# Giving product M5 of a GELU MLP its second Strassen level, with chained PSUM sums and claimed result tiles, on one Trainium2 core

## The chip, the cores and the metric

The kernel runs on one core of one Trainium2 chip. The metric is the device time of one execution in microseconds (us); a quoted time is the median of several executions. Every run quoted here is fast: the mean granted TensorE clock of a run was 0.996 or higher. Ratios are the mean time of one kernel's fast runs over that of the other's fast runs of the same rounds, so they are not quite the ratio of the medians beside them.

The engines are named as the profile names them: PE is TensorE (PEld its weight loads), DVE is VectorE, ACT is ScalarE, POOL is GpSimd, and SP is the engine whose queue issues the loads.

## The reference

```python
x: (8, 1024, 1024)   w1: (1024, 4096)   w2: (4096, 1024)   # float32
h = x @ w1
h = 0.5 * h * (1 + np.tanh(np.sqrt(2 / np.pi) * (h + 0.044715 * h ** 3)))
return (h @ w2).astype(np.float32)
```

## The kernel before

The 8192 rows are worked on in eight superblocks (SB 0 to 7) of 1024 rows. Each has a first matmul (`x @ w1`, then GELU, result `g` in fp16) and a second (`g @ w2`). Each of these is one level of Strassen's method: seven products M1 to M7 of half-size blocks in place of eight.

In the second matmul of SB 2 to 7 five of the seven products (M1, M2, M3, M6, M7) are split once more: an inner Strassen product makes seven quarter-size multiplications of 16 matmuls with 256 columns, so 112 x 256 columns instead of 64 x 512. M4 and M5 are still plain. A split product needs four more operand sums (made by VectorE during the product before it) and four more weight sums (made once, early, and kept in HBM as `in_d[m]`).

The inner product before, which the change rewrites; `ab`, `bb`, `cb` are PSUM banks, `tt` is a VectorE add or subtract, `act_copy` a ScalarE copy:

```python
def steps(self, into):
    ...
    ab, bb, cb = psum(), psum(), psum()
    self.multiply(1, ab, True);  v = temp(); act_copy(v, ab)              # step 1
    self.multiply(6, bb, True);  tt(c12, pair(v), pair(bb), ADD, True)    # 2
    self.multiply(2, ab, False); act_copy(c11, pair(ab))                  # 3
    self.multiply(7, bb, False); tt(c21, pair(v), pair(bb), ADD, True)    # 4
    self.multiply(5, cb, True);  tt(c22, c21, pair(cb), ADD, True)        # 5
    self.multiply(4, ab, True);  tt(c21, c21, pair(ab), SUB, True)        # 6
    self.multiply(3, cb, False); tt(c12, c12, pair(cb), ADD, True)        # 7
    # (cut: the storing of finished parts, the hand-over after each step, and, in the last
    # superblock, M7's base tile, with three more VectorE adds)
```

A third argument of False means that the matmuls add to what the bank holds. The order of VectorE's other jobs is a table, keyed by (product, step); a job runs after what that step itself gives VectorE to do. `x511` makes an operand block of M5, `a51` an operand sum of M5, the other letters add result tiles:

```python
FILL_2 = slots("""00:x122 x112 a11 a12 a13 a14 x222 x212 x622 x612 x621 x611
    ;12:a21;14:a22;15:a23;17:a24
    ;21:u0 u1;22:a31;23:u2 u3;24:a32;25:a33 d11;26:d22;27:a34 d21 d12
    ;32:g50;34:g51 e11;35:g52 e22;36:e21;37:g53 e12
    ;50:a61 x721;51:a62 x722;52:a63 x711;53:a64 x712
    ;64:a71;66:a72;67:a73;71:a74;72:n5;73:n1;74:n2;75:n7;76:n6""")
up = tile_pool(name="up", bufs=26)   # 26 buffers of 4 KB a partition: weights, blocks, result tiles
```

Each engine works through its own instructions in program order (for VectorE the 4.57 us of idle time shown below are the evidence). A tile of the `up` pool takes a buffer that an earlier tile has left, and its first writer waits for that tile's last user. The weight tiles of the next product are loaded into buffers that the product before last leaves, one after the other, as PE finishes with them.

## Time and profile before

| | before |
|---|---|
| time, median of 3 runs | 1528.28 us (1527.41 to 1528.83) |
| span of the profiled run | 1525.9 us |
| PE busy | 1517.1 us (99%) |
| first matmul of one of SB 2 to 7 | 96.69 us |
| second matmul of one of SB 2 to 7 | 88.75 us = 2 x 13.81 + 5 x 12.23 |

From the page of the kernel before: the span, then each engine's busy time, its share and its number of instructions.

```profile
span 1525.9 us, 22990 instructions
...
PE 1517.1 (99%) x8702; PEld 852.3 (56%) x8702; DVE 1073.8 (70%) x1354; ACT 486.3 (32%) x817; POOL 357.2 (23%) x380
```

PE is 99% busy. The chain of work that ended last shows what that is made of. It is listed in order of time: start in us, length in us, what. SB 3's second matmul and the first matmul before it:

```profile
594.78 96.69 PE ps L366 x448
691.48 13.81 PE ps L791 x64
705.29 36.68 PE ps L726 x336
741.97 13.81 PE ps L791 x64
755.78 24.45 PE ps L726 x224
```

Every piece is PE and there is no gap. L366 is the first matmul, L791 a plain product (M4 at 691.48, M5 at 741.97), L726 the split ones (three, then two). One plain product takes 13.81 us: 215.8 ns for each of its 64 matmuls. One split product takes 36.68 / 3 = 12.23 us: 109.2 ns for each of 112. That is the price list for the change.

From the windows view, M5 and the product after it; the columns are the window, then PE, PEld, DVE, ACT and POOL busy us with their counts of instructions, the clock, the DMA share and GB/s:

```profile
741.97:755.78 13.81, 13.81 (x67) 6.32 (x65) 11.89 (x14) 1.75 (x3) 5.68 (x10) 1.00 1.00 366
755.78:768.00 12.22, 12.22 (x115) 10.95 (x113) 7.86 (x10) 1.76 (x3) 3.68 (x6) 1.00 1.07 324
```

VectorE has idle time in both and the DMA engines are at a share of 1.0 already.

### The profile page before, as it was taken

To read this page: it belongs to the slowest core of one execution; us is meant where nothing else is said; L and a number is where in the kernel's file an instruction comes from. 1 tells how busy PE (TensorE), PEld (TensorE's weight loads), DVE (VectorE), ACT (ScalarE), POOL (GpSimd) and SP (SyncE) were. 2 spreads that over 40 slices of the span, in tenths; PEclk is the share of its full clock that TensorE was granted. 3 is DMA by queue.
4 is the path that set the end of the run, shared out by engine and by line. 5 is a ranking of instruction groups with operands and counts; after the bars stand their busy time and mean duration, and the time that the engine had idled before them with its cause. 6 is when DMAs were issued, how large, how long until landed. Compare 5 with 4: busy or idle time off the path is not lost.

```text
span 1525.9 us, 22990 instructions
## 1 busy us (share of the span) xinstructions
PE 1517.1 (99%) x8702; PEld 852.3 (56%) x8702; DVE 1073.8 (70%) x1354; ACT 486.3 (32%) x817; POOL 357.2 (23%) x380
## 2 busy tenths in 40 slices
PE   9999999999999999999999999999999999999999
PEld 4444444444444677446764477544875448744486
DVE  5876868768755787557875587656876567855786
ACT  6655024410144212442124411344113441144300
POOL 1242011211297022130212203131121400204011
PEclk9999999999999999999999999999999999999999
DMA  9999985894998899769996699966999769993697
GB/s 317 348 327 349 253 281 184 281 304 156 351 362 232 309 324 312 240 159 328 321 305 212 176 348 320 312 186 198 329 308 325 185 211 320 306 353 90 221 326 185
DMA packets 226191, 417.84 MB, mean 274 GB/s; under 512 B 78752, under 2 KB 85920, under 8 KB 225184
## 3 DMA queue, kind: packets, MB, share of 16 engines
q1 hardware_dynamic: 193536, 314.64, 61.4%
q0 software_dynamic: 32544, 101.73, 24.4%
q8 instruction: 68, 1.11, 0.3%
q14 instruction: 43, 0.35, 0.1%
HBM read 311.43 MB, written 119.54 MB: 282 GB/s over the span
## 4 chain that ended last, share of the span: by engine, by line
PE 85%; DVE 0%; issue 0%
PE ps L366 44%; PE ps L726 24%; PE ps L791 17%; DVE u L142 0%
## 5 line engine op out<-in xcount | busy, mean ns | idle before, releaser
L366 PE MATMUL ps<-u 128*128 128x512 f16 x3584 | 776.1, 379 | 3.6 <-DVE tmp L142 1.5
L366 PEld LDWEIGHTS <-u 128*128 128x128 f16 x3584 | 350.5, 98 | 427.1 <-issue 4.7
L142 DVE TENSOR_TENSOR tmp<-tmp,ps 128x512 f32<-128x512 f32 x528 | 361.7, 686 | 298.1 <-ACT tmp L430 114.6
L376 ACT ACTIVATE g<-tmp 128x512 f16<-128x512 f32 x256 | 161.1, 630 | 294.4 <-DVE tmp L142 294.3
L726 PE MATMUL ps<-u,gc 128*128 128x256 f16 x1920 | 224.3, 273 | 0.0
L142 DVE TENSOR_TENSOR u<-u 128x2048 f16<-128x2048 f16 (+3 forms) x233 | 211.9, 937 | 16.6 <-ACT u L321 11.7
L791 PE MATMUL ps<-u,gc 128*128 128x512 f16 x1024 | 222.6, 379 | 0.0
L726 PEld LDWEIGHTS <-gc 128*128 128x128 f16 x1920 | 187.9, 98 | 21.7
L376 ACT ACTIVATE g<-ps 128x512 f16<-128x512 f32 x256 | 151.4, 596 | 88.1 <-PE ps L366 87.9
L791 PEld LDWEIGHTS <-gc 128*128 128x128 f16 x1024 | 100.1, 98 | 119.6
L791 PE MATMUL ps<-u,g 128*128 128x512 f16 x640 | 139.8, 379 | 0.0
L490 POOL DMA_DIRECT2D out_dram<-u x58 | 58.5, 1019 | 311.2 <-DVE u L142 299.0
L142 DVE TENSOR_TENSOR u<-u,ps 128x512 f32<-128x512 f32 x131 | 89.7, 685 | 46.1 <-PE ps L791 17.0
L158 ACT COPY tmp<-ps 128x512 f32<-128x512 f32 x54 | 31.6, 585 | 272.1 <-PE ps L726 161.3
L469 POOL TENSOR_TENSOR u<-g,g 128x2048 f16<-128x2048 f16 x24 | 97.2, 4067 | 75.0 <-ACT g L376 60.1
L791 PEld LDWEIGHTS <-g 128*128 128x128 f16 x640 | 62.7, 98 | 75.5
L726 PE MATMUL ps<-u,g 128*128 128x256 f16 x864 | 103.1, 273 | 0.0
L478 POOL DMA_DIRECT2D out_dram<-u x52 | 39.0, 770 | 249.0 <-ACT u L158 227.3
L430 ACT COPY tmp<-ps 128x512 f32<-128x512 f32 x128 | 72.9, 569 | 69.7 <-PE ps L366 69.7
L142 DVE TENSOR_TENSOR tmp<-ps,tmp 128x512 f32<-128x512 f32 x128 | 88.3, 690 | 5.9 <-PE ps L366 1.2
L726 PEld LDWEIGHTS <-g 128*128 128x128 f16 x864 | 84.5, 98 | 11.1
L142 DVE TENSOR_TENSOR u<-tmp,ps 128x512 f32<-128x512 f32 x60 | 41.3, 688 | 63.9 <-PE ps L726 41.4
(42 smaller groups left out, 736.2 us busy)
## 6 DMA issues: line engine op xcount, KB each, us to landing
u<-w_d SPq DMA_DIRECT2D x384, 256.0 KB, 7.2
u<-in_d SPq DMA_DIRECT2D x120, 512.0 KB, 7.3
u<-raw_d SPq DMA_DIRECT2D x132, 256.0 KB, 6.6
out_dram<-u POOLq DMA_DIRECT2D x58, 512.0 KB, 9.0
u<-raw_d SPq DMA_DIRECT2D x56, 512.0 KB, 7.1
gc<-in_w_dram SPq DMA_DIRECT2D x48, 512.0 KB, 6.5
w_d<-u POOLq DMA_DIRECT2D x36, 512.0 KB, 4.2
raw_d<-u SPq DMA_DIRECT2D x32, 512.0 KB, 9.9
```

The costliest lines, as they stand in the source:

```text
L142: i = nc.vector.tensor_tensor(out=out, in0=in0, in1=in1, op=op)
L158: tc.keep_in_program_order(nc.scalar.copy(out=out, in_=in_))
L366: nc.tensor.matmul(bank, lhsT=ops[:, k, :], rhs=xs[m][:, k, :], start=(first and k == 0), stop=(k == KH - 1), skip_group_check=not first,)
L376: gelu_last[0] = nc.scalar.activation(out=g[b][:, c, :], in_=src, func=GELU)
L430: nc.scalar.copy(out=v, in_=pb)
L469: nc.gpsimd.tensor_tensor(out=early[m][b], in0=gu, in1=gv, op=SUB)
L478: return nc.gpsimd.dma_start(out=out2[r0:r0 + P, o0:o0 + OH], in_=src, **kw)
L490: return nc.gpsimd.dma_start(out=rows, in_=src, **kw)
L726: tc.keep_in_program_order(nc.tensor.matmul(bank[:, i * OH // 2:(i + 1) * OH // 2], lhsT=t[:, c, i * P:(i + 1) * P], rhs=self.y[j][:, c, : ...
L791: i = nc.tensor.matmul(pair(bank), lhsT=a[:, c, :], rhs=chunks(pieces[c // QC])[:, :, c % QC, :], start=(first and c == 0), stop=(c == NI ...
```

## The change

Its intent: M5's second matmul of SB 2 to 7 gets the second level too. That takes four things.

- The weight sums of M5 (`in_d[5]`) are made by VectorE in SB 1's first matmul.
- The inner sums chain in PSUM. Steps 1, 3, 5 and 7 all accumulate in one bank `a`, and its content is copied out after each by ScalarE. Only four VectorE adds are left in a product.
- Both result tiles of a product are claimed at its start by one-element ScalarE writes, before the next product's weight loads ask for buffers.
- VectorE's job table is arranged anew for the six split products, and GpSimd makes two more operand blocks ahead.

```diff
-    ;21:u0 u1;22:a31;23:u2 u3;24:a32;25:a33 d11;26:d22;27:a34 d21 d12
-    ;32:g50;34:g51 e11;35:g52 e22;36:e21;37:g53 e12
+    ;21:u0 u1;23:a31 u2;24:a32;25:a33;26:a34;27:u3 x511
+    ;31:x512;32:d11;33:a51;34:a52;35:a53;36:a54;37:d22 d21 d12
+    ;51:e11 e22;53:a61 e21;54:a62;55:a63;56:a64;57:e12 x721
+    ;61:x722 x711;62:x712 m11;63:a71;64:a72;65:a73 m22;66:a74;67:m21 m12
+    ;71:f11 f12;72:f21 f22;73:n5;74:n1;75:n2;76:n7;77:n6
     (cut: the other rows)
+            a, b, c = psum(), psum(), psum()
+            for n, (j, bank, first, out, adds) in enumerate((
+                (1, a, True, "11", ()),
+                (2, b, True, None, ("11",)),
+                (6, a, False, "12", ()),
+                (5, c, True, None, ("12",)),
+                (7, a, False, "22", (("22", c),)),
+                (3, b, True, None, ("12",)),
+                (4, a, False, "21", ()),
+            ), 1):
+                self.multiply(j, bank, first)
+                if out is not None:
+                    t = quarter(into, out)
+                    if self.base is None:
+                        act_copy(t, pair(bank))
+                    else:
+                        tt(t, quarter(self.base, out), pair(bank), ADD, True)
+                for o in adds: ...   # VectorE: tt(t, t, pair(ps), ADD, True)
+        def claim():
+            t = half()
+            act_copy(t[:, 0, :1], warm)
+            return t
         for m, after in zip(order, order[1:] + (None,)):
+            if m in products:
+                into[m] = [claim(), claim()]
             if after is not None:
-                load(after)
+                products[after].load()
     (cut: M5's plain product; the split of its weights in SB 1; in-place operand blocks)
```

In the last superblock M7 has a base to add, so there VectorE, not ScalarE, reads bank `a`.

More of the change, by code (lines that the diff above doesn't have):

```diff
@@ L52 @@
 FROM_2 = (2,)
-FROM_SUMS = (1, 3)
-INNER = MADE_INNER + FROM_2 + FROM_SUMS
+IN_M1 = ({}, {2: (5, 0), 8: (5, 1)}, {0: (1, 0), 2: (1, 1), 4: (3, 0), 6: (3, 1)})
+INNER = MADE_INNER + FROM_2 + (1, 3, 5)
 IN_PLACE = (6, 7)
@@ L65 @@
 W_TERMS = {1: "11", 2: "21", 3: "22"}
-W_SUMS = {1: (5, "12", SUB, "11"), 2: (6, "22", SUB, 1), 3: (7, "22", SUB, "12"), 4: (4, 2, SUB, "21")}
+W_SUMS = {1: (5, "12", SUB, "11"), 2: (6, "22", SUB, 1), 3: (7, "22", SUB, "12"), 4: (4, "21", SUB, 2)}
 S_TERMS = {1: "11", 2: "12", 4: "22"}
 S_SUMS = {1: (5, "21", ADD, "22"), 2: (6, 1, SUB, "11"), 3: (7, "11", SUB, "21"), 4: (3, "12", SUB, 2)}
-EARLY = ((1, "11"), (1, "21"), (2, "11"), (2, "21"))
-W_ORDER = (1, 6, 2, 7, 5, 4, 3)
+EARLY = ((1, "11"), (1, "21"), (2, "11"), (2, "21"), (6, "11"), (6, "21"))
+W_ORDER = (1, 2, 6, 5, 7, 3, 4)
 def slots(table):
@@ L77 @@
 FILL_2 = slots("""00:x122 x112 a11 a12 a13 a14 x222 x212 x622 x612 x621 x611
-    ;12:a21;14:a22;15:a23;17:a24
-    ;21:u0 u1;22:a31;23:u2 u3;24:a32;25:a33 d11;26:d22;27:a34 d21 d12
-    ;32:g50;34:g51 e11;35:g52 e22;36:e21;37:g53 e12
-    ;50:a61 x721;51:a62 x722;52:a63 x711;53:a64 x712
-    ;64:a71;66:a72;67:a73;71:a74;72:n5;73:n1;74:n2;75:n7;76:n6""".replace("\n    ", ""))
+    ;11:x522;13:a21;14:a22;15:a23;16:a24;17:x521
+    ;21:u0 u1;23:a31 u2;24:a32;25:a33;26:a34;27:u3 x511
+    ;31:x512;32:d11;33:a51;34:a52;35:a53;36:a54;37:d22 d21 d12
+    ;51:e11 e22;53:a61 e21;54:a62;55:a63;56:a64;57:e12 x721
+    ;61:x722 x711;62:x712 m11;63:a71;64:a72;65:a73 m22;66:a74;67:m21 m12
+    ;71:f11 f12;72:f21 f22;73:n5;74:n1;75:n2;76:n7;77:n6""".replace("\n    ", ""))
 @with_exitstack
@@ L279, in __init__, with make @@
             self[3], self[4] = blocks["11"], blocks["22"]
-        def make(self, *ms, cols=slice(None), pin=False):
+        def make(self, *ms, cols=slice(None), pin=False, over=False):
             for m in ms:
@@ L284, in make @@
                 if m not in self:
-                    self[m] = unit(KH, HT)
+                    self[m] = self.blocks[u] if over and m in IN_PLACE else unit(KH, HT)
                 tt(self[m][:, :, cols], self.blocks[u][:, :, cols], self.blocks[v][:, :, cols], SUB, pin)
@@ L384, in finish @@
             gelu("22", c, c22)
-        more = []
+        more, splits = [], []
         xb = [None]
-        early = {1: {}, 2: {}}
+        early = {1: {}, 2: {}, 6: {}}
         blocks = None
@@ L455, in matmul1 @@
                 ahead(q + 1, j)
-            if sb == 2 and c < 8 and c % 2 == 0:
-                split_on_pool(FROM_SUMS[c // 4], c // 2 % 2)
+            if sb < 3:
+                if c in IN_M1[sb]:
+                    splits += split_in_m1(*IN_M1[sb][c])
+                while splits and sb == 2:
+                    splits.pop(0)()
+                if c in (5, 6, 7, 8, 11, 12, 13, 14) and sb == 1:
+                    splits.pop(0)()
             if 1 < sb < NSB - 1:
@@ L464, in matmul1 @@
                     x_transpose(xb[0], load_in_order, blocks, range((c - 9) // 2, (c - 7) // 2))
-            if sb > 1 and c >= NI - 4:
-                m, b = EARLY[c - NI + 4]
-                early[m][b] = unit(NI // 2, HT // 2)
+            if sb > 1 and c >= NI - len(EARLY):
+                m, b = EARLY[c - NI + len(EARLY)]
                 gu, gv = (inner_block(g[t], b) for t in A_TERMS[m])
+                early[m][b] = gu if m in IN_PLACE else unit(NI // 2, HT // 2)
                 nc.gpsimd.tensor_tensor(out=early[m][b], in0=gu, in1=gv, op=SUB)
@@ L597, in prepare @@
             ops[i] = operand2(g, m, q, True)
-        fill = [lambda m=m: xs.make(m, pin=True) for m in (5, 1, 2, 7, 6)]
+        fill = [lambda m=m: xs.make(m, pin=True, over=True) for m in (5, 1, 2, 7, 6)]
         if sb:
@@ L652, in split_jobs, with split_in_m1, make @@
         return [lambda n=n: make(n) for n in W_SUMS]
-    def split_on_pool(m, h):
-        raw = []
+    def split_in_m1(m, h):
+        raw, t = [], {}
+        pool, name = (gcp, "gc") if m == 5 else (up, "u")
         for k in range(2):
-            raw.append(unit(2, HALF))
+            raw.append(pool.tile([P, 2, HALF], DT, name=name))
             q = 2 * k + h
             nc.sync.dma_start(out=flat(raw[k]), in_=stored(w2_d[q], raw2_d[q], m))
-        t = {}
-        for n, (_, u, op, v) in W_SUMS.items():
+        def make(n):
+            _, u, op, v = W_SUMS[n]
             if n % 2:
-                two = unit(2, HALF)
-            t[n] = two[:, (n + 1) % 2]
+                t["two"] = pool.tile([P, 2, HALF], DT, name=name)
+            t[n] = t["two"][:, (n + 1) % 2]
             in0, in1 = (
@@ L668, in split_on_pool @@
             )
-            nc.gpsimd.tensor_tensor(out=t[n], in0=in0, in1=in1, op=op)
+            if m == 5:
+                tt(t[n], in0, in1, op, True)
+            else:
+                nc.gpsimd.tensor_tensor(out=t[n], in0=in0, in1=in1, op=op)
             nc.gpsimd.dma_start(
@@ L672, in split_on_pool @@
             )
+        return [lambda n=n: make(n) for n in W_SUMS]
     def inner_block(t, b):
@@ L700, in load, with load_raw @@
                     nc.sync.dma_start(out=self.y[j], in_=in_d[self.m][:, n - 1])
-                    continue
-                k, b = (int(d) - 1 for d in W_TERMS[j])
-                for h in range(2):
-                    d = stored(w2_d[2 * k + h], raw2_d[2 * k + h], self.m)
-                    nc.sync.dma_start(
-                        out=self.y[j][:, h * QC:(h + 1) * QC, :].rearrange("p c n -> p (c n)"),
-                        in_=d[:, b * HALF:(b + 1) * HALF],
-                    )
+                else:
+                    self.load_raw(j)
+        def load_raw(self, j):
+            k, b = (int(d) - 1 for d in W_TERMS[j])
+            for h in range(2):
+                d = stored(w2_d[2 * k + h], raw2_d[2 * k + h], self.m)
+                nc.sync.dma_start(
+                    out=self.y[j][:, h * QC:(h + 1) * QC, :].rearrange("p c n -> p (c n)"),
+                    in_=d[:, b * HALF:(b + 1) * HALF],
+                )
         def make_x(self, b):
@@ L735, in steps @@
         def steps(self, into):
-            base = self.base
-            c11, c12, c21, c22 = (quarter(into, b) for b in ("11", "12", "21", "22"))
-            if base is not None:
-                b11, b12, b21, b22 = (quarter(base, b) for b in ("11", "12", "21", "22"))
-            ab, bb, cb = psum(), psum(), psum()
-            self.multiply(1, ab, True)
-            v = temp()
-            act_copy(v, ab)
-            yield 1
-            self.multiply(6, bb, True)
-            tt(c12, pair(v), pair(bb), ADD, True)
@@ L748, in steps @@
-            if base is not None:
-                tt(c12, c12, b12, ADD, True)
-            yield 2
-            self.multiply(2, ab, False)
-            if base is None:
-                act_copy(c11, pair(ab))
-            else:
-                tt(c11, b11, pair(ab), ADD, True)
-            self.part("11", c11)
-            yield 3
-            self.multiply(7, bb, False)
-            tt(c21, pair(v), pair(bb), ADD, True)
-            if base is not None:
-                tt(c22, c21, b22, ADD, True)
-                tt(c21, c21, b21, ADD, True)
@@ L763, in steps @@
-            yield 4
-            self.multiply(5, cb, True)
-            tt(c22, c21 if base is None else c22, pair(cb), ADD, True)
-            self.part("22", c22)
-            yield 5
-            self.multiply(4, ab, True)
-            tt(c21, c21, pair(ab), SUB, True)
-            self.part("21", c21)
-            self.rows(1, into[1])
-            yield 6
-            self.multiply(3, cb, False)
-            tt(c12, c12, pair(cb), ADD, True)
-            self.part("12", c12)
-            self.rows(0, into[0])
@@ L777, in steps @@
-            yield 7
+            a, b, c = psum(), psum(), psum()
[13 more added lines that the diff above has]
+                        act_copy(t, pair(bank))
+                    else:
+                        tt(t, quarter(self.base, out), pair(bank), ADD, True)
+                for o in adds:
+                    o, ps = o if isinstance(o, tuple) else (o, bank)
+                    t = quarter(into, o)
+                    tt(t, t, pair(ps), ADD, True)
+                for o, at in (("11", 2), ("22", 5), ("12", 6), ("21", 7)):
+                    if n == at:
+                        self.part(o, quarter(into, o))
+                if n > 5:
+                    self.rows(n - 6, into[n - 6])
+                yield n
@@ L814, in product2, with half @@
             yield q, banks[q]
+    def half():
+        return up.tile([P, 2, OH], F32, name="u")
     def halves():
-        tiles = [up.tile([P, 2, OH], F32, name="u") for _ in range(2)]
+        tiles = [half(), half()]
         return tiles, [tiles[q // 2][:, q % 2, :] for q in range(NQ)]
@@ L821, in matmul2 @@
         end = sb == NSB - 1
-        ops, pieces = {}, {}
         u2, u = halves()
-        into, rows = {}, {}
+        into = {}
         def out(o, **kw):
@@ L831, in matmul2 @@
             2: Inner(2, g, out("21", accum_op=ADD), x=early[2]),
-            3: Inner(3, g, out("12")),
-            6: Inner(6, g, out("22", accum_op=ADD)),
+            3: Inner(3, g),
+            5: Inner(5, g),
+            6: Inner(6, g, out("22", accum_op=ADD), x=early[6]),
         }
@@ L838, in matmul2 @@
             products[7] = Inner(7, g, out("11", accum_op=ADD))
-        def copy(q, ps):
-            t = temp()
-            act_copy(t, ps)
-            return t
         def post4(q, ps):
@@ L847, in post4, with add @@
             store(sb, "21", q, u[q])
-        def post5(q, ps):
-            store(sb, "12", q, copy(q, ps), accum_op=ADD)
-            tt(u[q], u[q], ps, SUB, True)
-            if not end:
-                store(sb, "11", q, u[q])
-        posts = {4: post4, 5: post5}
-        def load(m):
-            if m in products:
-                products[m].load()
-            else:
-                pieces[m] = load_pieces(m)
+        def add(o, m, b, op):
+            t = quarter(o, b)
+            tt(t, t, quarter(into[m], b), op, True)
         def run(key):
             for job in FILL_2.get(key, ()):
-                kind, m, i = job[0], int(job[1]), job[2:]
-                if kind == "x":
+                kind, b = job[0], job[1:]
+                m, i, a = int(b[0]), b[1:], int(b[0]) - 1
+                if kind == "x" and i not in products[m].x:
                     products[m].make_x(i)
@@ L869, in run @@
                     products[m].make(int(i))
-                elif kind == "g":
-                    ops[m, int(i)] = operand2(g, m, int(i), True)
                 elif kind == "u":
-                    tt(u[m], u[m], rows[1][m], ADD, True)
-                elif kind in "de":
-                    b = job[1:]
-                    d = quarter(into[1], b)
-                    tt(d, d, quarter(into[2 if kind == "d" else 3], b), SUB if kind == "d" else ADD, True)
-                    if job in ("e21", "e12"):
-                        a = int(b[0]) - 1
-                        store_rows(sb, "22", a, into[1][a])
-                elif nxt is not None:
-                    nxt.make(m, pin=True)
+                    tt(u[m], u[m], into[1][m // 2][:, m % 2, :], ADD, True)
+                elif kind == "d":
+                    add(into[1], 2, b, SUB)
+                elif kind == "e":
+                    add(into[1], 3, b, ADD)
+                    if b in ("21", "12"):
+                        store_rows(sb, "22", a, into[1][a])
+                elif kind == "m":
+                    add(u2, 5, b, SUB)
+                    if b in ("21", "12") and not end:
+                        store_rows(sb, "11", a, u2[a])
+                elif kind == "f":
+                    add(into[3], 5, b, ADD)
+                    if b in ("22", "12"):
+                        store_rows(sb, "12", a, into[3][a])
+                elif kind == "n" and nxt is not None:
+                    nxt.make(m, pin=True, over=True)
+        def claim():
+            t = half()
+            act_copy(t[:, 0, :1], warm)
+            return t
         order = (4, 1, 2, 3, 5, 6, 7)
-        load(4)
+        pieces = load_pieces(4)
         run((0, 0))
         for m, after in zip(order, order[1:] + (None,)):
+            if m in products:
+                into[m] = [claim(), claim()]
             if after is not None:
-                load(after)
+                products[after].load()
             if m in products:
-                into[m], rows[m] = halves()
                 for n in products[m].steps(into[m]):
@@ L896, in matmul2 @@
                 ps = psum()
-                a = ops.get((m, q))
-                matmuls2(ps, operand2(g, m, q) if a is None else a, pieces[m], True, pin=True)
-                posts[m](q, ps)
-                run((m, q))
+                matmuls2(ps, operand2(g, m, q), pieces, True, pin=True)
+                post4(q, ps)
     idle = consts.tile([P, HT], DT, name="idle")
```

## The prediction

> **What bounds the kernel.** TensorE. The page gives PE 1517.1 of 1525.9 us (99%) at full clock; the chain that ended last is PE from 219.3 to 1522.06 us; PE idles about 5 us in all, nearly all in the first 45 us. Only fewer or cheaper matmuls shorten it. In the chain in time order, each of the six later superblocks has a first matmul of 96.69 us and a second of 88.75 us: two plain products of 13.81 us (64 x 512 columns, 215.8 ns each) and five split ones of 12.23 us (112 x 256 columns, 109.2 ns each). This agrees with the Trainium skill, "TensorE: Matmul & The Clock Gate", Back-to-back issue gap (N/2.4 + 2.5 ns).
>
> **Removed.** M5's plain product becomes split: 13.81 - 12.23 = 1.585 us less PE in each of 6 superblocks, 9.5 us. Chaining leaves 4 VectorE adds (0.69 us) and 4 ScalarE copies (0.585 us) a product. One 1 MB accumulating store per superblock goes.
>
> **Added.** (a) VectorE in the second superblock's first matmul: 8 half-size subtractions (0.717 us), one a chunk; VectorE is 4.0 to 5.2 us busy in 5.83 us slices there, so the heaviest reach about 5.95: tight, but PSUM gives chunks of slack. (b) In the second matmul more VectorE operand jobs (1.22 us); product 6 then carries about 13.5 us of VectorE work in 12.2 us of PE. Starts of such jobs lie 1.13 us apart, so I estimate that its lag grows to about 3.4 us and is recovered in product 7. (c) Two more GpSimd subtractions (4.07 us) while GpSimd is idle. (d) 12 tiny ScalarE claims; ScalarE is 1.2 to 2.9 us busy per product. (e) M5 loads 3.67 MB instead of 2.1; the DMA share is already 0.92 to 1.07 in these windows. By the buffers' previous users, a load can start 12 to 19 us before PE wants it (7.3 us to landing): less lead than now, but enough.
>
> **On the critical path.** The 9.5 us, entirely. The new hazard is the chained bank: steps 1, 3, 5, 7 share it, and PE may not write it until it is read (the skill, "PSUM — Partial Sum Buffer", PSUM bank collisions raise a hardware error). The step between lasts 16 x 109.2 ns = 1.75 us against a 0.585 us ScalarE copy: no wait in five of six superblocks. In the last superblock product 7's bank is read by VectorE, behind a lag near 3.4 us: I estimate 1 us of PE stall, once. Late loads: 0 to 2 us in all.
>
> **Prediction: 1519.5 us**, 8 in 10 between 1517.5 and 1522.5: a gain of 0.57%. Chances: over 2% faster 0.01, within 2% 0.98, over 2% slower 0.01.
>
> **What would show it.** Right: split products in a row, no 13.81 us piece after product 4, second matmul about 87.2 us, PE busy down by 9.5 us, PE idle up by 0 to 2 us; the first 312 us unchanged. A step is wrong if PE waits for ScalarE copies behind a claim (blocked by a store that has not landed; most likely product 7's, whose tile waits for M1's result store); for DMA of weights in products 5 to 7; for VectorE in the last product by over 2 us; or in the second superblock's first matmul.
>
> **What would make it wrong.** DMA already saturated: less lead could become 1 to 3 us of PE wait per superblock, up to about 1528.

## The result, and the profile after

| | before | after |
|---|---|---|
| time, median | 1528.53 us (1527.41 to 1528.83, 4 runs) | 1521.22 us (1520.66 to 1522.10, 4 runs) |
| ratio of the fast runs | | 0.9954 (95% interval 0.9937 to 0.9971) |
| span of the profiled run | 1525.9 us | 1518.6 us |
| PE busy | 1517.1 us | 1508.3 us |
| second matmul, SB 2 to 6 | 88.75 us | 87.50 us |
| second matmul, SB 7 | 88.77 us | 87.60 us |

The time fell by 7.3 us (0.48%), inside the predicted range and 1.7 us above its middle. The page after:

```profile
span 1518.6 us, 23894 instructions
...
PE 1508.3 (99%) x8990; PEld 880.4 (58%) x8990; DVE 1097.6 (72%) x1392; ACT 526.7 (35%) x946; POOL 385.8 (25%) x366
```

The chain after, SB 3 again (L367 is the first matmul, L793 plain, L742 split):

```profile
690.35 13.81 PE ps L793 x64
704.17 31.45 PE ps L742 x288
735.62 0.02 issue
735.64 0.04 DVE u L143
735.68 1.11 issue
736.79 0.69 DVE u L143
737.48 0.04 issue
737.52 40.33 PE ps L742 x368
777.85 96.69 PE ps L367 x448
```

The second piece of 13.81 us is gone. The second matmul is 777.85 - 690.35 = 87.50 us. Six split products without a gap would take 73.36 us, so 87.17 us in all. The rest, 0.33 us, is one place: the chain leaves PE after 288 matmuls of split products (two products and four steps of the third), goes through VectorE and comes back. The same five lines stand in SB 2, 4, 5 and 6.

The timeline of that place in SB 2 shows why. Start, length, engine, line, operation, result and operands; in brackets the idle time before it and what ended it:

```profile
549.70 0.58 ACT L159 COPY u<-ps 128x512 f32<-128x512 f32 x1 [2.85 <-PE ps L742]
551.45 1.22 DVE L143 TENSOR_TENSOR u<-g,g 128x2048 f16<-128x2048 f16 x1 [4.57 <-PE ps L742]
552.60 0.68 DVE L143 TENSOR_TENSOR u<-u,ps 128x512 f32<-128x512 f32 x1
...
553.33 1.91 PE L742 MATMUL ps<-u,gc 128*128 128x256 f16 x16 [0.17 <-DVE u L143]
```

Product 3 began at 544.42. Its second step ended at 547.91 with VectorE due to add bank `b`. But the job before that add in VectorE's order, `x512` (the line at 551.45), was waiting: "4.57 <-PE" says that VectorE sat idle for 4.57 us until PE finished something, and that was step 4 of product 3 itself. (ScalarE was on time: its copy of bank `a` at 549.70 followed step 3 at once.) The add ran at 552.60 instead of just after 547.91. Step 6 of product 3 overwrites `b`, so PE had to wait for it. It lost 0.33 us against its pace; the 0.17 in the bracket is less, because the ends of the matmul records before it are modelled and reach into the gap (a record is 0.27 us long, and matmuls start 0.109 us apart). So the list of PE's waits gives the five places together only 0.8 us, for the 1.65 us that they cost:

```profile
PE ps L742 <- DVE u L143: 0.8, 5, 0.2
```

The windows view after, products 5 to 7 of SB 3:

```profile
741.16:753.40 12.24, 12.24 (x115) 10.98 (x113) 12.24 (x17) 2.52 (x6) 0.74 (x1) 1.00 1.03 362
753.40:765.60 12.20, 12.20 (x114) 10.93 (x113) 12.20 (x14) 2.52 (x6) 0.74 (x1) 1.00 1.02 337
765.60:777.85 12.25, 12.25 (x114) 10.93 (x112) 12.25 (x18) 2.52 (x6) 5.33 (x6) 1.00 1.07 304
```

VectorE, with time to spare before, now has none in these three products by its records, and the DMA share is 1.02 to 1.07. PE still does not wait there in SB 2 to 6.

**Balance.** Where PE's seamless run starts, in SB 1's first matmul, to PE's last matmul is 1522.06 - 219.28 = 1302.78 us before and 1514.74 - 219.12 = 1295.62 us after: 7.16 us less. The parts are 6 x 1.585 = 9.51 us of matmuls gone, 5 x 0.33 = 1.65 us of waits at `x512`, 0.43 us of waits in SB 7's last product, and 0.30 us in SB 1 (219.12 to 409.34 against 219.28 to 409.20). In sum: 9.51 - 1.65 - 0.43 - 0.30 = 7.13.

The first 219 us are left out because they scatter: that point lay between 218.7 and 221.1 us in the profiles, at 219.18 and 220.52 us in two kernels (experiments 1 and 10) whose programs are the same up to there.

### The profile page after: what moved, and what is told of

Read it like the earlier page. It is cut to its first block, busy times and chain, and to the rows that moved or that the text cites. A ratio compares the mean times of both kernels' runs of the same rounds, so it can differ in the third digit from the quotient of the medians.

```text
span 1518.6 us, 23894 instructions
## 1 busy us (share of the span) xinstructions
PE 1508.3 (99%) x8990; PEld 880.4 (58%) x8990; DVE 1097.6 (72%) x1392; ACT 526.7 (35%) x946; POOL 385.8 (25%) x366
## 4 chain that ended last, share of the span: by engine, by line
PE 84%; DVE 1%; issue 0%; DVEq 0%
PE ps L367 44%; PE ps L742 28%; PE ps L793 12%; DVE u L143 0%; DVE gc L143 0%; DVEq L143 0%
## 5 line engine op out<-in xcount | busy, mean ns | idle before, releaser
L367 PE MATMUL ps<-u 128*128 128x512 f16 x3584 | 776.4, 379 | 4.0 <-DVE tmp L143 1.8
L367 PEld LDWEIGHTS <-u 128*128 128x128 f16 x3584 | 350.6, 98 | 427.3 <-issue 5.2
L742 PE MATMUL ps<-u,gc 128*128 128x256 f16 x2304 | 258.3, 273 | 1.0 <-DVE u L143 0.8
L143 DVE TENSOR_TENSOR u<-u 128x512 f32<-128x512 f32 (+3 forms) x278 | 239.9, 900 | 16.9 <-ACT u L322 11.5
L742 PEld LDWEIGHTS <-gc 128*128 128x128 f16 x2304 | 225.4, 98 | 28.2 <-issue 2.0
L159 ACT COPY u<-ps 128x512 f32<-128x512 f32 x164 | 96.0, 585 | 405.8 <-PE ps L742 341.6
L496 POOL DMA_DIRECT2D out_dram<-u x68 | 66.6, 1262 | 396.8 <-DVE u L143 316.6
L793 PE MATMUL ps<-u,g 128*128 128x512 f16 x640 | 139.9, 379 | 0.0
L793 PE MATMUL ps<-u,gc 128*128 128x512 f16 x640 | 138.8, 379 | 0.0
L143 DVE TENSOR_TENSOR u<-u,ps 128x512 f32<-128x512 f32 x164 | 112.9, 688 | 35.5 <-PE ps L793 16.9
L793 PEld LDWEIGHTS <-gc 128*128 128x128 f16 x640 | 62.6, 98 | 75.5
L793 PEld LDWEIGHTS <-g 128*128 128x128 f16 x640 | 62.6, 98 | 75.5
L742 PE MATMUL ps<-u 128*128 128x256 f16 x864 | 99.2, 273 | 0.0
L742 PE MATMUL ps<-u,g 128*128 128x256 f16 x864 | 99.2, 273 | 0.0
L143 DVE TENSOR_TENSOR u<-g,g 128x2048 f16<-128x2048 f16 x48 | 57.5, 1222 | 49.6 <-PE ps L742 44.5
L742 PEld LDWEIGHTS <-u 128*128 128x128 f16 x864 | 84.5, 98 | 11.1
L742 PEld LDWEIGHTS <-g 128*128 128x128 f16 x864 | 84.5, 98 | 9.8
```

Source lines behind the costliest of these rows:

```text
L143: i = nc.vector.tensor_tensor(out=out, in0=in0, in1=in1, op=op)
L159: tc.keep_in_program_order(nc.scalar.copy(out=out, in_=in_))
L367: nc.tensor.matmul(bank, lhsT=ops[:, k, :], rhs=xs[m][:, k, :], start=(first and k == 0), stop=(k == KH - 1), skip_group_check=not first,)
L496: return nc.gpsimd.dma_start(out=rows, in_=src, **kw)
L742: tc.keep_in_program_order(nc.tensor.matmul(bank[:, i * OH // 2:(i + 1) * OH // 2], lhsT=t[:, c, i * P:(i + 1) * P], rhs=self.y[j][:, c, : ...
L793: i = nc.tensor.matmul(pair(bank), lhsT=a[:, c, :], rhs=chunks(pieces[c // QC])[:, :, c % QC, :], start=(first and c == 0), stop=(c == NI ...
```

## The experiments

Theory A for the shortfall: no buffer of `up` is free when `x512` comes up, so it waits for a weight tile of product 3 to be used up, and since VectorE is in order the read of bank `b` comes late. Rival B: the DMA engines are saturated and weights land late, or ScalarE's copies are late behind the claims.

### 1. The waiting job moved behind the add

```diff
-    ;31:x512;32:d11;33:a51
+    ;32:d11 x512;33:a51
```

> The changed kernel with one operand job moved: VectorE makes M5's 12-block after the add that reads product 3's second bank, not before it. Theory A (no free buffer: the job waits until product 3's own fourth weight tile is used up, VectorE is in order, so the bank is read late and PE waits 0.33 us at product 3's sixth step in each of five superblocks): those five waits vanish, 1.65 us less, about 1519.5 us; the last superblock's 0.43 us stays. Rival B (weights land late or DMA is saturated, or ScalarE copies are late behind claims): unchanged, 1521.2.

Measured: 1520.22 us (1518.98 to 1521.35, 5 runs; ratio to before 0.9946). The chain of this kernel, SB 3:

```profile
690.08 13.81 PE ps L793 x64
703.89 73.36 PE ps L742 x672
777.25 96.69 PE ps L367 x448
```

All six split products run in one piece of 672 matmuls and 73.36 us; the same in SB 2 and 4 to 6. All five waits are gone, and PE's run from SB 1 on is 1513.16 - 219.18 = 1293.98 us, 1.64 less than after the change. That is the size that theory A gave. The medians differ by 1.0 us only, with runs that scatter over 2 us, so the profile and not the clock carries this verdict.

### 2. and 3. One buffer more, one buffer less

```diff
-    up = ...(name="up", bufs=26)      tp = ...(name="tp", bufs=10)
+    up = ...(name="up", bufs=27)      tp = ...(name="tp", bufs=8)     # e2
+    up = ...(name="up", bufs=25)      tp = ...(name="tp", bufs=10)    # e7
```

> The changed kernel with 27 buffers in the large pool instead of 26, paid for by 8 instead of 10 of the small temporaries; the job order is that of the change. Theory A: by the built program the job's buffer is then that of product 3's third weight tile, free 1.75 us earlier, so VectorE reads the bank in time: the same 1519.5 as with the job moved. Rival B: 1521.2, or a little less if more buffers mean earlier loads in general. Fewer temporaries could cost a little in the first matmuls; no wait of PE for them is expected.

> The changed kernel with 25 buffers in the large pool. Theory A: by the built program the job's buffer is that of product 3's fifth weight tile, free 1.75 us later than in the changed kernel; PE's wait at product 3's sixth step grows from 0.33 to about 2.1 us in each of five superblocks, so about 9 us slower than the changed kernel, 1530. Rival B (loads late): stalls of other sizes, at DMA semaphores in products 5 to 7, or hardly any change.

Measured: with 27 buffers 1520.32 us (ratio to before 0.9942), and the chain again has unbroken pieces of 672 matmuls in SB 2 to 6; in SB 3:

```profile
704.66 73.36 PE ps L742 x672
```

With 25 buffers 1544.08 us (4 runs, ratio 1.0108). So a buffer more cures the wait without any move of the job: the shortage is the cause. For 25 buffers, who waited for whom (total us, times, longest us), first PE and then its weight loads, which have a list of their own:

```profile
PE ps L367 <- DMA u<-w_d: 9.8, 10, 1.7
PE ps L742 <- DVE u L143: 9.6, 5, 1.9
```

```profile
PEld L367 <- DMA u<-w_d: 14.7, 10, 2.2
```

The second line is theory A's: five waits at product 3's sixth step, 9.6 us. In the changed kernel the same list has 0.8 us for these five (shown above). That is 1.76 us more each, the one step that I had counted. But 25 buffers cost 23 us over the changed kernel, and the expectation of 1530 missed by 14. In the profiled run PE's time from SB 1 on is 21.9 us longer than in the changed kernel. Of this 8.8 us are the five waits, and 1.7 us are a clock effect: for 3.41 us from 1355.6 on the granted clock was half, and SB 7's first matmul lost that much (94.20 us for 428 matmuls, against 92.55 in SB 3 to 6). The rest, 11.4 us, are loads of the next first matmul's weights (`w_d`) that came late. The chain of that run, from SB 2 to SB 3:

```profile
584.23 1.21 DVE u L143 x2
...
585.98 8.02 DMA out_dram<-u
...
594.14 0.32 SPq L257
...
594.51 7.68 DMA u<-w_d
...
602.24 92.55 PE ps L367 x428
```

Read it upward from the end: PE waited for weights whose load took 7.68 us; the load could start only when a store of results had landed (8.02 us) and left its buffer; and the store waited for two VectorE adds. Is this rival B, too little lead for the DMA, or does it come from VectorE?

### 4. One buffer less, and the job moved

The edits of experiments 1 and 3 together.

> 25 buffers in the large pool and the job moved as in the first experiment. Takes the 23 us that 25 buffers cost apart. If the two parts add (PE held by VectorE at product 3's sixth step, 9.6 us of waits in all; PE's weight loads held by late weights at the start of the next first matmul, 14.7 us): the first part goes and the second stays, 1534 to 1536. If the late weights follow from VectorE's delay in product 3: both go and the time is near 1521.

Measured: 1521.78 us (ratio to before 0.9957); on the same chip and in the same rounds the changed kernel itself had 1521.87. The whole list of PE's waits in this run:

```profile
PE ps L367 <- DVE tmp L143: 4.0, 3, 2.6
PE ps L367 <- DVE u L143: 1.5, 1, 1.5
PE ps L296 <- DVE warm L907: 1.2, 1, 1.2
PE ps L367 <- ACT g L377: 0.2, 1, 0.2
```

No split product (L742) waits, and no matmul waits for `w_d`. (What the list has, L367 and L296, lies in the first 125 us, in SB 0, where the kernels before and after have such waits too.) So the late weights were a consequence too: 1544.08 - 1521.78 = 22 us hung on where one job of 1.2 us stood in VectorE's order (1.7 us of it, in the profiled run, is the half clock of experiment 3, whose cause no run shows). PE does not wait for loads even with 25 buffers, as long as VectorE is not held.

One small wait is left that the list hides, since it leaves out idle times under 0.15 us. In the chain of this run, at the start of SB 3's first matmul:

```profile
598.14 0.69 DVE tmp L143
598.83 0.04 issue
598.87 93.40 PE ps L367 x432
```

That first matmul takes 96.98 us instead of 96.69, and so do those of SB 4 to 7: VectorE comes to its first add there about 1 us later, measured against PE, than in experiment 1, and PE loses 0.29 us each time. With 25 buffers the moved job is therefore not quite free: PE's time from SB 1 on is 1.5 us longer than in experiment 1.

### 5. and 6. The second level on M5 without the chained sums

Steps as in the kernel before, with the changed kernel's other parts and the job of experiment 1 moved; the last operand sum of each product one step later, because the old order keeps its buffer that long.

```diff
-            a, b, c = psum(), psum(), psum()
-            for n, (j, bank, first, out, adds) in enumerate(( ...
+            ab, bb, cb = psum(), psum(), psum()
+            self.multiply(1, ab, True)
+            v = temp()
+            act_copy(v, ab)
+            ... (as before; the sign of the fourth weight sum follows the change)
-W_ORDER = (1, 2, 6, 5, 7, 3, 4)
+W_ORDER = (1, 6, 2, 7, 5, 4, 3)
```

> M5 split as in the change, with the job of the first experiment moved, but each split product's sums are made as before the change (two more VectorE adds from a second bank, one ScalarE copy to a temporary). If chaining is what lets M5's split pay (VectorE has about 0.7 us less a product): VectorE reads the second bank of products 5, 6, 7 late and PE waits at their fourth step, by my count about 2.4 us a superblock, 12 to 18 us in all: about 1533, no faster than the kernel before. If chaining is only tidiness (PE bound): 1519.5 to 1521.

Measured: 1552.22 us (4 runs, ratio 1.0157), slower than expected. Its trace showed PE held behind two jobs that wait for buffers, so I moved these as well (`x522` from step 1 to step 3 of product 1, `x512` to step 4 of product 3):

> The unchained kernel of before with its two operand jobs that wait for a buffer (M5's blocks, in products 1 and 3) moved behind the bank reads that they held up, to where their buffers are free. Of the 1552 us of the unchained kernel some was due to these two: in the trace PE waited 1.9 us behind the first of them and about 1.3 us behind the second, in each superblock. If nearly all of it came from them, this lands at 1520 to 1525 and chaining is worth little by itself; if the rest is VectorE's larger load in products 5 to 7 with only one step of room, as I had counted (2.4 us a superblock), it lands at 1530 to 1538.

Measured: 1536.54 us (6 runs, 1532.85 to 1540.16, ratio 1.0053). The profiled run is the fastest of the six; why others took up to 7 us more, no trace shows. Who waited for whom, first the unchained kernel, then the one with later jobs:

```profile
PE ps L742 <- DVE u L143: 24.1, 21, 1.9
```

```profile
PE ps L742 <- DVE u L143: 10.1, 17, 1.3
```

In the later one the second matmul of SB 2 is 596.22 - 506.80 = 89.42 us, 2.24 us above an unbroken one; I had counted 2.4. The agreement is partly luck: I had counted waits in products 5, 6 and 7, and PE lost 0.45 us in product 5, 1.44 in product 6, none in product 7, and 0.32 in product 3. So the second level on M5 without the chained sums is slower than the kernel before, by 8 us at the job table that I found. The extra VectorE work is small (1120.7 us busy in all against 1099.4 in the changed order with the job moved; 36 more instructions, so one add more in each of the 36 products, where the expectation says two), but without chaining bank `bb` is written at step 2 and again at step 4. VectorE must read it within one step, 1.75 us, and with operand jobs in its queue it did not: PE waited up to 1.3 us at a time. In the chained form ScalarE reads the bank that is reused every second step, and VectorE's bank `b` is reused only four steps later. A better table for the unchained form may exist.

### 7. The chained sums alone

The kernel before with the chained steps, the weight order and the sign that they need; M5 plain, no claims. Two adds of result tiles stood before the step that now finishes their quarter. They were swapped (`36:e12;37:g53 e21`).

> The kernel before with one part of the change alone: the chained sums (with the weight order and the sign that they need); M5 stays plain, no claims. Theory: PE never waited in the second matmul before, so less VectorE work buys nothing there: 1528.3 within 1 us, VectorE busy down by some 20 us. Rival (chaining saves time by itself): 1525 or less.

Measured: 1527.88 us, ratio to before 0.9998 (0.9985 to 1.0010). VectorE is 1058.0 us busy instead of 1073.8, and the second matmul is 88.76 us in SB 2 to 6, as before. Chaining gains nothing by itself. With the job tables tried here, it is what makes room for the rest (experiments 5 and 6).

### 8. Without the claims

```diff
-                into[m] = [claim(), claim()]
+                into[m] = [half(), half()]
```

(with the job of experiment 1 moved)

> The first experiment's kernel (job moved) with the one-element ScalarE writes left out, so that a result tile takes its buffer at its first real copy, after the next product's weights have taken theirs. Theory: the claims matter because ScalarE's copy frees the chained bank. By the built program product 3's first result tile then waits for the end of that product's second step, so ScalarE's copy ends about 0.7 us into PE's third step, and product 5's waits for VectorE's work on product 2's sums: 0.7 to 2 us of PE wait a superblock, 4 to 12 us in all, 1524 to 1532. Rival (claims only tidy the order, ScalarE has time to spare): 1520.

Measured: 1523.70 us (1522.80 to 1524.46, ratio 0.9971), 3.5 us more than the same kernel with claims. The timeline of product 3 in SB 2:

```profile
547.78 0.59 ACT L159 COPY u<-ps 128x512 f32<-128x512 f32 x1 [2.91 <-PE ps L742]
...
548.41 1.80 PE L742 MATMUL ps<-u,gc 128*128 128x256 f16 x15 [0.67 <-ACT u L159]
```

ScalarE's first copy of the product waited until step 2 was over (547.75 in the chain), because, by the built program, its tile had taken the buffer of a weight tile that PE still read (in the kernel of experiment 1 the same copy began at 546.32, although PE was 0.24 us later there); and PE's third step waited 0.67 us for that copy. Without the claim the loads of the next product had taken the free buffers first. The second matmul is 593.99 - 505.98 = 88.01 us, 0.83 us above an unbroken one. The same 88.01 us stands in SB 3 to 6. The wait that I had expected in product 5 as well did not come, so the result lies just under the expected 1524 to 1532.

### 9. M5's weights split by GpSimd

```diff
-            if m == 5:
-                tt(t[n], in0, in1, op, True)
-            else:
-                nc.gpsimd.tensor_tensor(...)
+            if True:
+                nc.gpsimd.tensor_tensor(...)
```

(with the job of experiment 1 moved)

> The first experiment's kernel with M5's weight split in the second superblock made by GpSimd, not VectorE (8 subtractions of about 2.1 us on an engine 15% busy there). Theory: either engine hides it, PE does not wait in that first matmul: 1520.2 within 0.7 us. Rival: VectorE near its limit there costs time, so GpSimd is faster by 0.3 us or more; or GpSimd's queue of stores is held up and PE waits, slower by over 1 us.

Measured: 1522.78 us (1522.31 to 1527.49, ratio 0.9970), 2.6 us more than with VectorE. My theory fell, and so did both rivals in the form that I gave them. The timeline in SB 1's first matmul:

```profile
234.40 4.28 DVE L143 TENSOR_TENSOR u<-u 128x2048 f16<-128x2048 f16 x2
...
235.13 5.54 POOL L678 TENSOR_TENSOR gc<-gc 128x1024 f16<-128x1024 f16 x2
...
239.33 1.02 PE L367 MATMUL ps<-u 128*128 128x512 f16 x4 [1.26 <-DVE tmp L143]
```

Two VectorE subtractions of 128x2048 fp16 from SBUF, 1.22 us each elsewhere, took 4.28 us together while GpSimd worked on its own subtractions; the longest single one took 3.15 us. The f32 adds that come after them in VectorE's order were held, and PE waited (1.26 us at 239.33). The Trainium skill describes this ("SBUF — State Buffer", sections Who interferes with whom and Summary: rules for kernel authors): a VectorE instruction with two SBUF inputs and a GpSimd instruction that reads SBUF exclude each other, and the one that issues second blocks until the first has finished. The trace agrees: the VectorE subtraction that took 3.15 us instead of 1.22 started at 235.53, while GpSimd worked on one from 235.13 to 237.59, and ended 1.1 us after it; GpSimd's next one then took 3.10 us instead of 2.14. VectorE's own split costs 8 x 0.685 us and holds PE for 0.30 us in all. It is the better engine here, although it is the busier one.

### 10. A version without PE waits

Experiment 1, and six adds (the expectation miscounts them) moved behind bank reads of product 7, for SB 7, where VectorE reads the chained bank:

```diff
-    ... 66:a74;67:m21 m12
-    ;71:f11 f12;72:f21 f22;73:n5;74:n1;
+    ... 66:a74
+    ;71:m21 m12;73:f11 f12 n5;74:f21 f22 n1;
```

> The first experiment's kernel with four adds and four adds moved behind product 7's first and third bank reads (M5's last two subtractions after step 1, the sums of M3 and M5 after steps 3 and 4). In the last superblock VectorE itself reads product 7's chained bank, 3 us behind PE at product 7's start; with fewer jobs before those reads the 0.43 us of PE wait there should go: 1519.8, and no wait of PE in any second matmul. If M5's and M3's stores then land too late at the end, the tail after PE's last matmul grows instead (3.1 us now).

Measured: 1519.61 us (ratio to before 0.9941). The chain, SB 7's second matmul to the end:

```profile
1426.89 13.81 PE ps L793 x64
1440.70 73.37 PE ps L742 x672
...
1514.17 0.69 DVE u L143
```

SB 7's wait of 0.43 us is gone too, the second matmul takes 87.18 us everywhere, and PE's list of waits (of 0.15 us and more) has none after the first 125 us. Then the changed kernel and this one side by side on one chip:

> The changed kernel once more, unaltered, so that it stands on the same chip as the next one: 1521.2 within 0.7 us by every theory. In the profile again five waits of PE at product 3's sixth step.

> The kernel with the later jobs once more, on the same chip as the changed kernel: by the profiles it has 2.0 us less of PE's time from the second superblock on (1293.6 against 1295.6), so a median 1 to 2.5 us under the changed kernel's. If the gain was only scatter of the start, whose first 220 us differed by up to 1.4 us between profiles, under 0.7 us.

Measured: 1521.87 us (ratio 0.9957, 0.9944 to 0.9971) and 1519.86 us (ratio 0.9943, 0.9930 to 0.9955), 2.0 us apart, as the profiles say; the changed kernel's trace shows the five waits again. The intervals against the kernel before overlap, so the times alone are weak evidence for so small a gain; the unbroken chain in both profiles of this version is strong evidence. By its profiles this is the kernel with the least PE time (1293.6 us from SB 1 on, against 1294.0 in experiments 1 and 2, whose times can't be told from it), 0.6% under the kernel before.

## Why the prediction was right or wrong

- **The bound and the gain: right.** PE bound the kernel; the split of M5 removed 1.585 us in each of six superblocks, as costed from 13.81 and 12.23 us. (PE's busy sum fell by 8.8 us, not by 9.5: half of each 0.33 us wait is covered by the modelled ends of records and counts as busy, and the first 219 us scatter.)
- **"No wait in five of six superblocks": wrong, the step that failed.** It considered only ScalarE's reads of the chained bank. There it was right: PE waited for no ScalarE copy in a second matmul of the changed kernel. VectorE's read of the other bank, `b`, was held up for 4.57 us by a job without a buffer, which cost 0.33 us in each of SB 2 to 6, 1.65 us together. Experiments 1 and 2 removed it in two independent ways. This is the size of the 1.7 us by which the result lay above the middle, while the smaller items partly cancel: 1 us expected and 0.43 met in SB 7, 0.30 in SB 1, no late loads. What the prediction says of the hazard itself, that PE may not write a bank until it has been read, shows in the traces as PE's waits for VectorE's read of `b`; that an unguarded write raises an error is not shown by any run here.
- **"I estimate 1 us of PE stall, once" in the last superblock: right in place and cause, too large.** It was 0.43 us; VectorE was about 2.9 us behind, not 3.4, and moving jobs away from there (experiment 10) removed it.
- **"Late loads: 0 to 2 us": none.** PE waited for no weights in a second matmul of the changed kernel. "Up to about 1528" did not happen, and experiment 4 shows that the loads had more room than I feared.
- **SB 1, "tight, but PSUM gives chunks of slack": nearly right.** PE did lose 0.30 us there, in three places, which the prediction's own list counts as a failed step. Experiment 9 shows that the other engine would not have been hidden.
- **The claims** were listed as a danger. They are the opposite: without them (experiment 8) a second matmul takes 0.83 us more.
- **Product 6 overloading VectorE: right.** VectorE's records fill the windows of products 5 to 7, and the lag is paid back.

## What to carry to other kernels

When PE is 99% busy, a cut in matmuls pays in full only as long as every bank is read before its next write is due: count for each bank how many steps lie between its read and its next write, and give the short distances to the engine with slack. A job that must wait for a buffer blocks everything behind it on an in-order engine, so place it behind the reads that release PE; here the position of one such job was worth 1.6 us with 26 buffers and about 22 us with 25. And claim result buffers before prefetches take them: here a prefetch could wait for a buffer that comes free late, and a bank read could not (0.83 us a superblock without the claims).

## What the Trainium skill lacked or had wrong

- "TensorE: Matmul & The Clock Gate", section Back-to-back issue gap: its formula N/2.4 + 2.5 ns agrees (215.8 ns at 512 columns and 109.2 at 256, over hundreds of matmuls in a row, each with its weight load). The sentence beside it, that a real stream of weight loads and matmuls sustains about 131 ns at N=512, does not: 96.69 us for 448 matmuls is 215.8 ns each.
- "GPSIMD Engine Reference", section Engine selection: it puts GpSimd at about 2x slower for two-input elementwise work, with no data type beside it. For fp16 subtractions from SBUF to SBUF the traces show 4.07 us against 1.22 (128x2048) and 2.14 against 0.69 (128x1024): 3.1 to 3.3 times.
- "SBUF — State Buffer", section Who interferes with whom: agrees (3.15 us for a 1.22 us VectorE subtraction beside GpSimd ones). What no page puts a number to is what that costs a bound PE behind it: 2.6 us here for eight GpSimd subtractions.
